# RWKV score products: each head's 64 rows alone, the two heads in turn, in place of 128 zero-padded rows

## The chip, the cores and the metric

The kernel is one program on one core of a Trainium2 chip. It has five instruction streams: PE (TensorE, matrix products; the profile shows its weight loads apart as PEld), DVE (VectorE), ACT (ScalarE), POOL (GpSimd) and SP (SyncE, which here issues nearly all DMA transfers). The metric is the device time of one execution in microseconds; less is better. The time of a kernel is the median of several runs.

## The reference

Two transformer blocks run one after the other on the same activations: 272 tokens with retention, mLSTM and 16 experts of 2816 hidden units, then 256 tokens with a gated delta net ("gdn" below), an RWKV-7 branch and 32 small experts. The second block also runs both branches over 256 context tokens, only for the state that they leave. The change is in the RWKV branch, which is this recurrence over 8 heads of 64 channels, in two directions:

```python
def rwkv7_scan(r, w, k, v, a, b, s0):
    '''S_t = S_{t-1} (diag(w_t) + a_t b_t^T) + v_t k_t^T ; y_t = S_t r_t.'''
    def step(s, inp):
        r_t, w_t, k_t, v_t, a_t, b_t = inp
        sa = jnp.einsum('...vk,...k->...v', s, a_t)
        s = s * w_t[..., None, :] + sa[..., :, None] * b_t[..., None, :] + v_t[..., :, None] * k_t[..., None, :]
        return s, jnp.einsum('...vk,...k->...v', s, r_t)
    s_fin, y = lax.scan(step, s0.astype(jnp.float32), xs)

    y, s_fin = rwkv7_scan(both_dirs(r_h), per_dir(heads(decay)), per_dir(k_dir), both_dirs(v_h),
                          both_dirs(-kk), per_dir(b_dir), s0)
```

It is run once on the context (state only, no y) and once on the 256 latent tokens, starting from the context's state.

## The kernel before

The sequence of 256 is cut in 4 chunks of 64 steps. Two heads share the 128 partitions: a pair j (0 to 3) has head h = 0 on partitions 0 to 63 and head h = 1 on 64 to 127; in the code `r` is a head's own half and `ro` the other one. For each pair and direction d:

- `rwkv_prep` and `rwkv_scale` project and scale keys, values and queries. They leave `ld` (the scaled −kk), `lw` (the scaled query, latent only), and `BK`, which holds for each chunk three blocks of 64 columns: scaled b, scaled k, scaled b again. `BK[:, c, h:h + 2, :]` is therefore (b, k) for head 0 and (k, b) for head 1.
- `rwkv_front` makes the chunk's inner products. `T[:, h, c]` is the moving operand of head h: 64 columns of `ld`, in the latent pass 64 of `lw`, and 64 of an identity that transposes. Its rows outside the head's half have to be zero, since the product contracts over all 128 partitions. Only the first 64 columns are overwritten later, so POOL sets them to zero again in each front (line 1598), DVE and ACT copy `ld` and `lw` in (lines 1599 and 1601), and PE multiplies (line 1612) into a bank `b` of PSUM that holds 4 chunks (context) or 2 (latent). Then the bank is emptied with masks: to `N` (line 1615), to the other half of `T` (line 1616), to `MR` (line 1618, latent), all on DVE, and to `BKt` on ACT (line 1619).
- `rwkv_back` inverts a unit triangular matrix made from N (`mixed_inverse`; its first products are `r0ic` and `r1ic`, line 1154, for d = 0 and 1) and walks the four chunks, each with the products of lines 1645, 1652, 1660, 1667 and 1675.

An fp32 product is two passes of the array: in the trace each matmul instruction appears as two MATMUL and two LDWEIGHTS records, in the order listings as one.

The context pass is a generator (`ctx_pre`) that runs inside the first block's experts: after a pair of expert matmuls (lines 892 and 910), `paced` advances it by as many `yield`s as are due, 470 for the first 1000 of 1050 pairs; what is left runs behind them. In the context d = 0 and d = 1 follow each other on the same tiles, with `T` in one buffer, and both use the two PSUM banks of "pb". In the latent pass d = 0 has the two banks of "pa" and d = 1 the two of "pc"; `hop(...)` (that is `fill`) issues steps of other work, projections (line 1093) and gdn products (`gic`, `gib`, `giy`), right behind the matmul that it is given, and `run` drains the generators, so that yields mean nothing there. The instructions of all this are put in their final order on each engine by a scheduler of the framework, which goes by what depends on what and by its own estimate of times. An engine then runs its list in that order. The lines of the loop in question:

```python
        for h, r, ro in self.HALF:
            for c0 in range(0, 4, cg):
                ...
                for i in range(cg):
                    ins = nc.tensor.matmul(b[:, i], BK[:, c0 + i, h:h + 2, :], T[:, h, c0 + i, :, :], start=True, stop=True)
                hop(0, HOPS[1])(ins)
```

Of the kernel before, what the change touches and what calls it, by code (L numbers as in the profile page):

```python
# [58 lines left out]
HOPS = 4, 1, (3, 1), (2, 1), (2, 1), (2, 1), (0, 4), (0, 4)  # L59
# [95 lines left out]
class Ring(list):  # L155
# [3 lines left out]
    def tile(self, *args, **kw):  # L159
        self.turn += 1  # L160
        return self[self.turn % len(self)].tile(*args, **kw)


class Net:
# [1419 lines left out]
    def rwkv_front(self, j, d, x, env):  # L1584

        nc = self.nc
        W, lat, na = env["W"], env["lat"], env["na"]
        nd = d if lat else 0
        T, N = env["T1"][nd], env["Ne"][nd]
        self.ptag = env["tags"][d]  # L1590
        ch = lambda ap: ap.rearrange("p (c t) -> p c t", c=4)
        rw = self.ct("rw").rearrange("p (d h a c) -> p d h a c", d=2, h=2, a=2)
        ld, lw, BK, wc, ic = x["scaled", d]
        tile = lambda shape, name: W.tile(shape, F32, name=f"{name}{nd}")
        hop = (lambda *steps: (lambda ins: self.fill(ins, *steps))) if lat and d == 0 else lambda *steps: (lambda ins: None)
        SU = tile([P, 2, 4, 64], "rSU")
        for h, r, ro in self.HALF:
            nc.gpsimd.memset(T[ro, h, :, 0, :], 0.0)
            nc.vector.tensor_copy(T[r, h, :, 0, :], ch(ld)[r])  # L1599
            if lat:  # L1600
                nc.scalar.copy(T[r, h, :, 1, :], ch(lw)[r])
            nc.gpsimd.tensor_scalar(SU[ro, h], x["vn"][ro], 1.0, 0.0, op0=ALU.mult, op1=ALU.add)

        BKt = tile([P, 2, 4, 64], "rKt")
        MR = tile([P, 2, 4, 64], "rMR") if lat else None
        cg = 2 if lat else 4
        for h, r, ro in self.HALF:
            for c0 in range(0, 4, cg):
                b = self.bank("rmt")[:, :cg * na * 64].rearrange("p (c a t) -> p c a t", c=cg, a=na)
                cs = slice(c0, c0 + cg)  # L1610
                for i in range(cg):
                    ins = nc.tensor.matmul(b[:, i], BK[:, c0 + i, h:h + 2, :], T[:, h, c0 + i, :, :], start=True, stop=True)  # L1612
                hop(0, HOPS[1])(ins)
                m = lambda rr, a: rw[rr, d, h, a:a + 1, :].to_broadcast([rr.stop - rr.start, cg, 64])
                nc.vector.tensor_mul(N[r, cs, r], b[r, :, 0, :], m(r, 0))
                nc.vector.tensor_mul(T[ro, h, cs, 0, :], b[ro, :, 0, :], m(ro, 0))
                if lat:
                    nc.vector.tensor_mul(MR[:, h, cs, :], b[:, :, 1, :], m(slice(0, P), 1))
                nc.scalar.copy(BKt[:, h, cs, :], b[:, :, na - 1, :])
                yield  # L1620
        return T, N, SU, BKt, MR, wc, ic

    def rwkv_back(self, j, d, x, front, env):
# [643 lines left out]
```

## Time and profile before

| | |
|---|---|
| three runs | 2544.38, 2549.94 and 2558.76 us, median 2549.94 |
| profiled execution | 2547.35 us, of which the span from first to last instruction is 2545.3 |
| TensorE clock granted, mean over the span | 0.958 of full |
| busy: PE, PEld, DVE, ACT, POOL | 2322.3, 1243.8, 1041.2, 653.8, 460.1 us |
| matmul of line 1612 | 256 records, 51.3 us busy |
| DMA | 755.05 MB, 297 GB/s over the span |

In time the program is: the first mixer (to about 300 us), the experts of the first block with the context pass inside (to 1738 us), the latent mixing stage (to about 2180 us), merging and the 32 small experts (to the end). The fronts of the change stand at 986 to 1635 us (8 of the context) and 1784 to 2096 us (8 of the latent pass). A busy share tells little by itself: matmuls are pipelined, and a record's end is modelled, so that the distance between starts is the better measure of what an instruction costs PE.

### The profile page before, as it was taken

The numbers are of one execution on the slowest core, as the hardware profiler recorded it, in microseconds if no ns is written. First come the engines' busy times: TensorE is split into PE (matmuls) and PEld (weight loads), VectorE is DVE, ScalarE is ACT, GpSimd is POOL, SyncE is SP. The second block draws the span as 40 slices with busy tenths as digits, with TensorE's granted clock in tenths as the row PEclk, the third lists the DMA queues.
The fourth block names the chain that finished last, engine by engine and source line by source line (L and its number), as shares of the span: only waits on it lengthen the run. The fifth ranks groups of instructions, "written<-read, shape, count | busy, mean of one in ns | idle before, by whom it ended". The sixth has DMA issues, their size and how long they took to land. (4 is left out here: it accounts for less than half of the span.)

```text
span 2545.3 us, 45033 instructions
## 1 busy us (share of the span) xinstructions
PE 2322.3 (91%) x18624; PEld 1243.8 (49%) x18624; DVE 1041.2 (41%) x2419; ACT 653.8 (26%) x1652; POOL 460.1 (18%) x657
## 2 busy tenths in 40 slices
PE   6879799999999999999899999997988999989997
PEld 5656533333333433333333333335766777865554
DVE  7786312232222312322322313223676464645545
ACT  4335111221121112212212112213443343522222
POOL 5672100000000101101101101103243342300000
PEclk9979899999999999999999999998888989999999
DMA  6547799999998999999999999996211112689995
GB/s 214 182 143 246 269 403 403 402 400 368 406 378 326 394 366 381 406 390 378 406 376 387 373 404 400 389 407 196 74 43 46 44 27 68 216 271 362 368 365 189
DMA packets 328176, 755.05 MB, mean 297 GB/s; under 512 B 13088, under 2 KB 167376, under 8 KB 324896
## 3 DMA queue, kind: packets, MB, share of 16 engines
q1 hardware_dynamic: 326464, 747.67, 79.5%
q0 software_dynamic: 1504, 4.46, 0.6%
q8 instruction: 149, 2.44, 0.4%
q14 instruction: 59, 0.48, 0.1%
HBM read 751.03 MB, written 1.05 MB: 295 GB/s over the span
## 5 line engine op out<-in xcount | busy, mean ns | idle before, releaser
L892 PE MATMUL gu<-w,xs 128*64 128x512 f32 (+1 forms) x3072 | 679.6, 570 | 1.6 <-DMA w<-in_w_up 1.3
L910 PE MATMUL dn<-w,hT 128*64 128x512 f32 x1408 | 336.6, 604 | 19.1 <-ACT hT L318 17.4
L892 PEld LDWEIGHTS gu<-w,xs 128*64 128x64 f32 x3072 | 195.6, 137 | 285.5 <-issue 270.6
L1093 PE MATMUL pc<-luT,w 128*128 128x256 f32 x688 | 180.7, 404 | 1.7 <-ACT r1iZ L1173 1.1
L910 PEld LDWEIGHTS dn<-w,hT 128*64 128x64 f32 x1408 | 88.8, 137 | 164.2 <-issue 131.6
L1093 PEld LDWEIGHTS pc<-luT,w 128*128 128x128 f32 x688 | 128.0, 197 | 19.7 <-ACT rSU L1664 1.2
L2123 PE MATMUL egu<-w,exs 128*64 128x256 f32 x1024 | 123.2, 383 | 0.0
L898 DVE TENSOR_TENSOR hid<-hid,gu 128x512 f32<-128x512 f32 (+1 forms) x48 | 30.7, 640 | 201.5 <-ACT hid L303 198.6
L1093 PE MATMUL pc<-cuT,w 128*128 128x256 f32 x288 | 99.2, 429 | 0.0
L1093 PEld LDWEIGHTS pc<-cuT,w 128*128 128x128 f32 x288 | 43.2, 188 | 107.8 <-issue 104.3
L2123 PEld LDWEIGHTS egu<-w,exs 128*64 128x64 f32 x1024 | 74.6, 136 | 39.4 <-issue 6.9
L1656 POOL TENSOR_SCALAR rsw<-rSU,rwc 64x64 f32<-64x64 f32 x112 | 39.8, 355 | 293.3 <-DVE rSU L1672 283.3
L301 ACT ACTIVATE hid<-gu 128x512 f32<-128x512 f32 (+1 forms) x48 | 26.9, 560 | 235.3 <-PE gu L892 235.3
L296 PE MATMUL pj<-uTh,wp 128*128 128x272 f32 x320 | 69.0, 310 | 10.7 <-DVE rtmp L469 6.4
L899 DVE TENSOR_TENSOR hid<-hid,gu 128x512 f32<-128x512 f32 (+1 forms) x48 | 30.8, 642 | 108.7 <-PE gu L892 107.1
L1612 PE MATMUL rmt<-rT,rBK 128*128 128x128 f32 (+1 forms) x256 | 51.3, 341 | 21.0 <-DVE rT L1599 13.9
L2150 PE MATMUL edn<-w,ehT 128*64 128x512 f32 x256 | 67.7, 597 | 0.7 <-ACT ehT L318 0.5
L286 ACT CAST wp<-w 128x1024 fp32r<-128x1024 f32 (+1 forms) x48 | 55.3, 1185 | 49.4 <-DMA w<-in_w_in 31.1
L287 DVE TENSOR_TENSOR wp<-w,wp 128x1024 fp32r<-128x1024 f32 (+1 forms) x44 | 62.3, 1441 | 12.2 <-ACT wp L286 12.1
L1439 POOL TENSOR_TENSOR rtm<-rpd 128x256 f32<-128x256 f32 x25 | 16.0, 640 | 273.5 <-ACT rpd L1437 264.5
L1028 POOL TENSOR_TENSOR adac<-adac,w 128x2048 f32<-128x2048 f32 x14 | 64.3, 4595 | 0.3
L1279 POOL TENSOR_TENSOR gx<-gx,gcv 128x256 f32<-128x256 f32 x20 | 14.5, 725 | 266.2 <-ACT gx L303 240.1
(680 smaller groups left out, 3678.2 us busy)
## 6 DMA issues: line engine op xcount, KB each, us to landing
w<-in_w_down SPq DMA_DIRECT2D x176, 1024.0 KB, 11.2
w<-in_w_gate SPq DMA_DIRECT2D x128, 1024.0 KB, 10.4
w<-in_w_up SPq DMA_DIRECT2D x128, 1024.0 KB, 12.1
w<-in_w_gate SPq DMA_DIRECT2D x64, 768.0 KB, 10.5
w<-in_w_up SPq DMA_DIRECT2D x64, 768.0 KB, 7.5
w<-in_w_in SPq DMA_DIRECT2D x65, 512.0 KB, 4.2
w<-in_moe_w_gate SPq DMA_DIRECT2D x32, 1024.0 KB, 13.4
w<-in_moe_w_up SPq DMA_DIRECT2D x32, 1024.0 KB, 12.0
```

What stands on the lines that cost most here:

```text
L286: self.nc.scalar.copy(hi, src)
L287: (eng or self.nc.vector).tensor_sub(lo, src, hi)
L296: self.nc.tensor.matmul(out, a[x], b[y], start=(i == 0 and x + y == 0), stop=(i == n - 1 and x == 1))
L892: ins = nc.tensor.matmul(b[h * 64:(h + 1) * 64, :w], xs[:, k, :], ws(k, slice(h * w, (h + 1) * w)), start=(k == 0), stop=(k == KD - 1))
L899: nc.vector.tensor_mul(hid, hid, gu[1][:, :w])
L910: ins = nc.tensor.matmul(dn[dc * 64:(dc + 1) * 64], hT[:, j, h * 64:(h + 1) * 64], wd(h * nf + j, slice(dc * 512, (dc + 1) * 512)), start= ...
L1028: nc.gpsimd.tensor_add(acc[c], acc[c], w)
L1093: self.nc.tensor.matmul(b, w(k), uT[:, k, :], start=(k == 0), stop=(k == KD - 1))
L1612: ins = nc.tensor.matmul(b[:, i], BK[:, c0 + i, h:h + 2, :], T[:, h, c0 + i, :, :], start=True, stop=True)
L1656: nc.gpsimd.tensor_scalar(sw[r], SU[r, h, c, :], wc[r, c:c + 1], 0.0, op0=ALU.mult, op1=ALU.add)
L2123: nc.tensor.matmul(b[64 * i:64 * i + 64, x * 256:x * 256 + 256], xs[:, k, i, :], w[i](k), start=(k == 0), stop=(k == KD - 1))
L2150: nc.tensor.matmul(b[64 * i:64 * i + 64, :], hT[:, j, 64 * i:64 * i + 64], wd[i](j, cs), start=(j == 0), stop=(j == 1))
```

## The change

The memset of line 1598 goes. The products of a head contract over its own 64 partitions only (`BK[r, ...]`, `T[r, ...]`), so that the stationary operand is 64 rows by 128 columns, in rows 0 to 63 of the array for head 0 and 64 to 127 for head 1. The loops are turned: for each group of chunks both heads' banks are taken at once, the matmuls are written chunk by chunk with the heads in turn, one `hop` of two steps stands behind all of them, then both banks are emptied, head 0 first. There is one yield for each group of chunks instead of one for each bank, that is 1 instead of 2 in a front of the context.

```diff
         for h, r, ro in self.HALF:
-            nc.gpsimd.memset(T[ro, h, :, 0, :], 0.0)
             nc.vector.tensor_copy(T[r, h, :, 0, :], ch(ld)[r])
...
-        for h, r, ro in self.HALF:
-            for c0 in range(0, 4, cg):
-                b = self.bank("rmt")[:, :cg * na * 64].rearrange("p (c a t) -> p c a t", c=cg, a=na)
-                cs = slice(c0, c0 + cg)
-                for i in range(cg):
-                    ins = nc.tensor.matmul(b[:, i], BK[:, c0 + i, h:h + 2, :], T[:, h, c0 + i, :, :], start=True, stop=True)
-                hop(0, HOPS[1])(ins)
+        for c0 in range(0, 4, cg):
+            cs = slice(c0, c0 + cg)
+
+            bs = [self.bank("rmt")[:, :cg * na * 64].rearrange("p (c a t) -> p c a t", c=cg, a=na) for _ in range(2)]
+            for i in range(cg):
+                for h, r, ro in self.HALF:
+                    ins = nc.tensor.matmul(bs[h][:, i], BK[r, c0 + i, h:h + 2, :], T[r, h, c0 + i, :, :], start=True, stop=True)
+            hop(0, 2 * HOPS[1])(ins)
+            for h, r, ro in self.HALF:
+                b = bs[h]
                 m = lambda rr, a: rw[rr, d, h, a:a + 1, :].to_broadcast([rr.stop - rr.start, cg, 64])
                 nc.vector.tensor_mul(N[r, cs, r], b[r, :, 0, :], m(r, 0))
                 nc.vector.tensor_mul(T[ro, h, cs, 0, :], b[ro, :, 0, :], m(ro, 0))
                 if lat:
                     nc.vector.tensor_mul(MR[:, h, cs, :], b[:, :, 1, :], m(slice(0, P), 1))
                 nc.scalar.copy(BKt[:, h, cs, :], b[:, :, na - 1, :])
-                yield
+            yield
```

PE's order in the fourth front of the context, before. `rmt` with its number is a bank of the product (of the two here the smaller number is head 0), `gu` and `dn` are the experts' banks, `r0ic` the first product of the inverse.

```order
L910 MATMUL dn_8090<-w_8202,hT_8194 64x512 x4
L1612 MATMUL rmt_8265<-rT0_6140,rBK0_8246 128x128 x4
L892 MATMUL gu_8273<-w_8274,xs_7851 64x512 x4
L1612 MATMUL rmt_8286<-rT0_6140,rBK0_8246 128x128 x4
L892 MATMUL gu_8273<-w_8276,xs_7851 64x512 x4
L1154 MATMUL r0ic_8309<-r0iB_8299 32x32 x16
```

The same place now:

```order
L903 MATMUL hb_8220<-ctab_64,hid_8214 128x128 x4
L910 MATMUL dn_8101<-w_8227,hT_8225 64x512 x4
L1612 MATMUL rmt_8243<-rT0_6140,rBK0_8205 128x128 x4
L1612 MATMUL rmt_8244<-rT0_6140,rBK0_8205 128x128 x4
L910 MATMUL dn_8101<-w_8229,hT_8225 64x512 x4
L910 MATMUL dn_8101<-w_8231,hT_8225 64x512 x4
L1154 MATMUL r0ic_8274<-r0iB_8264 32x32 x16
```

The eight products stand together, the four of head 0 ahead of the four of head 1; the heads are not in turn. Seven of the eight fronts of the context read so.

PE's order in the last front of the context, now:

```order
L892 MATMUL gu_10750<-w_10753,xs_10345 64x512 x2
L1612 MATMUL rmt_10791<-rT0_6140,rBK0_10774 128x128
L1612 MATMUL rmt_10792<-rT0_6140,rBK0_10774 128x128
L1612 MATMUL rmt_10791<-rT0_6140,rBK0_10774 128x128
L1612 MATMUL rmt_10792<-rT0_6140,rBK0_10774 128x128
L1612 MATMUL rmt_10791<-rT0_6140,rBK0_10774 128x128
L1612 MATMUL rmt_10792<-rT0_6140,rBK0_10774 128x128
```

Here alone the heads are in turn, as the loop writes them (the two rows that follow go on in the same way).

PE's order in the latent front of pair 1, d = 0, before. `rp13` and `rp24` are banks of the walk over the chunks, `pc` a projection, `gic` a product of the gdn inverse. The four banks of a front are, by rising number, head 0 with chunks 0 and 1, head 0 with 2 and 3, then head 1 in the same way; of them two are shown.

```order
L1675 MATMUL rp13_12651<-rSU0_12086,rMR0_12096 64x64
L1612 MATMUL rmt_12984<-rT0_11707,rBK0_12522 128x192 x2
L1093 MATMUL pc_12675<-luT_11601,w_11646 128x256
L1154 MATMUL gic_15474<-giB_15427 32x32 x2
L1645 MATMUL rp13_12883<-rSU1_12132,rT1_11708 64x64 x2
L1612 MATMUL rmt_12992<-rT0_11707,rBK0_12522 128x192 x2
L1093 MATMUL pc_12675<-luT_11601,w_11646 128x256
L1154 MATMUL gic_15474<-giZ_15428,giB_15427 32x32 x13
```

The same place now; by rising number the banks are head 0 and head 1 with chunks 0 and 1, then head 0 and head 1 with 2 and 3:

```order
L1677 MATMUL rp13_12631<-rSU0_12070,rMR0_12078 64x64
L1612 MATMUL rmt_12962<-rT0_11691,rBK0_12502 128x192 x2
L1647 MATMUL rp13_12863<-rSU1_12114,rT1_11692 64x64
L1154 MATMUL gic_15442<-giB_15395 32x32 x13
L1612 MATMUL rmt_12963<-rT0_11691,rBK0_12502 128x192 x2
L1093 MATMUL pc_12655<-luT_11585,w_11630 128x256 x2
...
L1612 MATMUL rmt_12978<-rT0_11691,rBK0_12502 128x192 x2
L1612 MATMUL rmt_12979<-rT0_11691,rBK0_12502 128x192 x2
L1093 MATMUL pc_12655<-luT_11585,w_11630 128x256 x2
```

A bank's two products still stand together, and other products mostly stand between the two heads' banks; in this front the second group has them next to each other.

## Rows read from the trace of the kernel before

**Rows 1.** Busy time by stretch: length, five engines (instructions), clock, DMA share, GB/s.
```profile
core 0: us, PE busy (x) PEld busy (x) DVE busy (x) ACT busy (x) POOL busy (x), PEclk, DMA share, GB/s
1440.00:1460.00 20.00, 18.38 (x204) 6.97 (x202) 6.01 (x16) 2.55 (x8) 2.63 (x4) 0.93 0.85 318
...
1500.00:1520.00 20.00, 19.15 (x84) 6.30 (x82) 1.25 (x3) 0.60 (x1) 0.48 (x2) 1.00 1.03 409
...
1720.00:1740.00 20.00, 14.96 (x77) 4.70 (x73) 3.19 (x6) 2.91 (x6) 0.97 (x1) 0.99 1.07 363
```

**Rows 2.** PE's waits, 330 to 1740 us: for whom, us in all, times, longest.
```profile
PE rmt L1612 <- DVE rT L1599: 13.9, 6, 3.1
...
PE r0ic L1154 <- POOL r0iB L1169: 3.0, 3, 1.7
...
PE gu L892 <- DMA w<-in_w_up: 1.3, 3, 0.5
```

**Rows 3.** Timeline of PE, two fronts of the context: start, length, what, records.
```profile
1252.17 1.16 PE L1612 MATMUL rmt<-rT,rBK 128*128 128x128 f32 x8
...
1253.26 1.94 PE L892 MATMUL gu<-w,xs 128*64 128x512 f32 x8
...
1375.12 2.05 PE L1612 MATMUL rmt<-rT,rBK 128*128 128x128 f32 x16
1377.10 4.09 PE L892 MATMUL gu<-w,xs 128*64 128x384 f32 x24
```

**Rows 4.** Timeline of PE: 64-row products in turn, and a stream of 128-row ones.
```profile
1666.54 0.73 PE L924 MATMUL sc<-yhi,ohT 64*128 64x512 f32 x4 [0.69 <-ACT yhi L918]
1667.20 1.08 PE L892 MATMUL gu<-w,xs 128*64 128x512 f32 x4
...
2294.70 4.10 PE L2084 MATMUL exg<-eohq,exp 128*128 128x256 f32 x32
2298.64 0.38 PE L2114 MATMUL ecb<-ctab,eohp 128*128 128x128 f32 x2
```

**Rows 5.** Groups of PE, 1745 to 2180 us: records, busy us, mean ns, idle before.
```profile
L1093 PE MATMUL pc<-luT,w 128*128 128x256 f32 x622 | 165.5, 406 | 1.1 <-ACT r1iZ L1173 1.1
L1612 PE MATMUL rmt<-rT,rBK 128*128 128x192 f32 x128 | 32.7, 391 | 7.2 <-ACT rT L1601 4.4 <-ACT rKt L1619 2.8
```

**Rows 6.** PE's waits, 1740 to 2180 us.
```profile
PE rp L1645 <- DVE rSU L1672: 8.0, 5, 4.3
PE rp L1675 <- DVE rSU L1664: 6.8, 4, 5.0
```

**Rows 7.** Timeline of all engines in the latent front of pair 1.
```profile
1882.96 0.92 PE L1612 MATMUL rmt<-rT,rBK 128*128 128x192 f32 x4
...
1883.72 0.59 PE L1093 MATMUL pc<-luT,w 128*128 128x256 f32 x2
...
1884.37 0.28 DVE L1615 TENSOR_TENSOR rN<-rmt,stab 64x128 f32<-64x128 f32 x1
...
1884.67 0.29 DVE L1616 TENSOR_TENSOR rT<-rmt,stab 64x128 f32<-64x128 f32 x1
...
1884.97 0.29 DVE L1618 TENSOR_TENSOR rMR<-rmt,stab 128x128 f32<-128x128 f32 x1
```

**Rows 8.** Busy time by stretch, latent stage, columns as in rows 1.
```profile
1797.80:1865.80 68.00, 65.10 (x820) 50.79 (x818) 37.34 (x95) 34.52 (x96) 17.74 (x32) 1.00 0.33 88
...
1893.30:1906.80 13.50, 13.50 (x214) 10.22 (x215) 7.53 (x28) 4.57 (x15) 5.29 (x12) 0.50 0.15 40
1958.20:1975.00 16.80, 11.72 (x80) 8.74 (x80) 12.80 (x29) 4.73 (x14) 6.45 (x8) 0.50 0.11 31
2006.00:2012.60 6.60, 5.39 (x53) 4.03 (x54) 3.40 (x10) 0.46 (x2) 0.45 (x1) 0.50 0.01 2
```

**Rows 9.** The memset of line 1598: ns min/median/max; what POOL waited for before it.
```profile
L1598 POOL MEMSET rT<- x32: 304/306/450, 887.0 to 2083.8; 64x256 f32 x32
...
  PE rp L1645: 13.2, 10
```

## The prediction, on record before the changed kernel ran

> **What bounds the kernel now.** I read the busy time by stretch first, for which engine or queue is full where, then PE's waits in the two stages that the change touches, then the timeline around single fronts, and last the granted clock of the latent stage.
>
> The experts of the first block, with the context pass among them, run between two full resources. Where nothing disturbs, PE is busy 19.15 of 20 us and DMA moves 409 GB/s at a share of 1.03; where a context front and the inverse behind it stand, DMA falls to 318 GB/s and 0.85, since PE frees weight buffers late; in the last 20 us of the stage, with the context done, PE is busy only 14.96 and DMA is full [rows 1]. Over the whole stage PE waits 1.3 us for weights, but 13.9 us, six times, for the copy into T ahead of the product, and 3.0 us for the first product of the inverse [rows 2]. So a microsecond that PE saves in a context front is part of a stage whose end waits for weights: some of it comes through, not all.
>
> In the latent stage little is loaded (88 GB/s in one stretch) and PE is busy 65.10 of 68 us [rows 8]; what it waits for are single late steps of the chunk walk, 8.0 and 6.8 us in all [rows 6]. There PE's time counts nearly in full. What matters as much is its clock: three stretches of 6.6 to 16.8 us were granted 0.50, the lower of its two levels (1.2 GHz), beside 68 us at 1.00 (2.4 GHz) [rows 8].
>
> **The change, part by part.** The first question is what a product costs. A front's 16 records of 128 columns take from 1375.12 to 1377.10 us, 1.98 us, and 8 of them from 1252.17 to 1253.26, 1.09 us [rows 3]. Two equations: 0.111 us a record and 0.20 us for entering and leaving. In the latent pass 4 records of 192 columns take 0.76 us until the next product starts [rows 7], 0.19 each; by columns from the context's it would be 0.167 (an estimate, 192/128 of 0.111). All 128 latent records are 32.7 us busy [rows 5], some of them at the lower clock.
>
> Contracting over 64 rows in place of 128 removes no record and no column. Time is gained only if the two halves of the array work at once. That this can be so is in the trace [rows 4]: four passes of 64 rows, halves in turn, 512 columns each, take from 1666.54 to 1667.20, 0.66 us. The passes over 128 rows with operands of the same type take 3.94 us for 32 of 256 columns, 0.123 each, so four of 512 would take 0.98 one after the other.
>
> But the order that PE gets decides whether neighbours lie in different halves, and it is not the loop's. The scheduler puts a bank's products together: in seven of the eight context fronts four of head 0, then four of head 1; in every latent front two of one head, then, mostly behind other work, two of the other. Products of one head use the same rows and follow each other. Only at a seam, where the last of head 0 stands next to the first of head 1, can two overlap.
>
> - Seams. Context: 7 fronts, one product (two records) hidden in each, 7 x 2 x 0.111 = 1.6 us; the last front alternates, 8 x 0.111 = 0.9. Sum -2.5 us. Latent: PE's list has three places where the heads' banks touch, 3 x 2 x 0.167 = -1.0 us.
> - Visits. A context front was two visits to PE between expert products, now it is one; one of the eight was one before. 7 x 0.20 = -1.4 us. In the latent fronts I count neighbours with another tile shape in PE's list: 31 at either end of the product's rows before, 56 now, since a projection, 128 by 128, was of the same shape and no longer is. Over the whole stretch from the first front to the last the list changes shape 357 times before and 356 now. So the price lies between 0 and 25 x 0.10 = 2.5 us (half a visit each); I take +1.0.
> - The drain. The Trainium skill, TensorEngine Tiling (Array Packing), section Tiling Modes, says that changing the tiling mode, unlike changing the tile, drains TensorE; the 0.20 us from [rows 3], between products of 64-column tiles, agree. By the rule as it stands the 25 added edges all pay; by the count over the whole list none is added.
> - Waits in the context. Between the products of `rbw` and a front's first product the list now has up to 12 expert products where it had 8 or 10, in three of the fronts, and a pair of them is worth about 0.9 us (half of the 1.94 us in [rows 3]). 13.9 us [rows 2] could shrink by 3; against that one front has only four expert products ahead of its inverse in place of ten. Bounds -3 and +3, taken -1.0.
> - Emptying. The same six DVE operations for a pair of banks, 0.28 to 0.29 us each [rows 7], and the ACT copies. Head 0's half of N is complete after the third bank and no longer after the second; the inverse needs both heads, and head 1 was last before too. Taken 0. If the last two banks come together, three operations of head 0 stand ahead of head 1's N: 0.9 us a front, +7 us over the eight latent fronts if nothing else were late; PE has other products to run meanwhile, which is what hides it.
> - The memset. 32 x 0.306 = 9.8 us of POOL go, and 13.2 us in which POOL stood before it, waiting for a product [rows 9]. What stood behind it on POOL, copies into SU and the scaling `rsw`, waits for the same walk over the chunks. Bounds 0 and -5, taken -0.3.
> - The generator. Eight fewer yields of the context end it some 17 expert pairs earlier (8 of 470 steps of 1000 pairs). That lengthens the stretch in which PE waits for weights anyway [rows 1]: 0.
>
> Sum. Context on PE: -2.5 - 1.4 - 1.0 = -4.9 us, of which I pass on a quarter, since the stage ends on full DMA [rows 1]: -1.2. Latent: -1.0 + 1.0 - 0.3 = -0.3. Together -1.5 on the profiled execution's 2547.35 us: 2545.9, said as 2546. That execution is 2.6 us below the median of the three runs, 2549.94, whose spread is 14 us. I call 0.5%, 12.7 us, what a measurement of this kernel can tell from no change, so faster means below 2537.2 and slower above 2562.7.
>
> **The rivals.**
>
> The halves overlap after all. If the array ran both heads side by side as the loop writes it, a context front would lose 8 x 0.111 = 0.9 us and the latent fronts 64 x 0.167 = 10.7 us, more at the lower clock. For it: the four passes of [rows 4], and the latent stage pays PE's time in full. Against it: the order. With a quarter of the context's 8 x 0.9 + 1.4 = 8.6 us, and the latent sum, it gives 2547.35 - 10.7 - 2.2 = 2534.
>
> The clock, which is the rival on the slower side. A latent stretch of 13.5 us at 0.50 in which PE has work, such as 1893.30 to 1906.80 with PE busy throughout [rows 8], costs half its length, 6.75 us. It begins just behind a latent front. Products on half the rows, and a list in which 25 more edges break the stream, could make PE look less active there. One stretch more gives 2553, two 2559, three 2566; it decides from the third on. Against it: as many columns pass as before, and the stretches at 0.50 may as well become fewer, by which the same step gives 2539.
>
> The drains and the late N. All 25 edges at 0.20 us, 5 us, and a part of the 7 us of emptying: 2552. For it: the 0.20 us of [rows 3]. Against it: the unchanged count over the list.
>
> **How the numbers follow.** No overlap but at seams, 2546: 0.58 (of it 0.05 faster, 0.02 slower, by a shuffled latent order). Overlap, 2534: 0.14 (0.10 faster, the rest within). Clock, 2553 to 2566: 0.13 (0.10 slower). Drains, 2552: 0.15 (0.01 slower). Faster 0.15, same 0.72, slower 0.13. The range takes in the overlap's 2534 and the clock's second step: 2534 to 2560. The likeliest case's own range is 2539 to 2553, one stretch of the clock either way.
>
> **What would show it.** The records of line 1612: still 256, now of shape 64 by 128. In a context front the start of the next product stands about 1.75 us behind the first (16 records less two, and one visit); 1.1 us would show the overlap, as it should in the last front. In the latent pass two products of one head should still take 0.6 us or more. Wrong would be the forecast if the product's busy time fell by a third or more in the latent stage, if the stretches at 0.50 there grew by more than two, or if PE's waits for DMA at the end of the experts moved that stage's end by over 5 us.

## The result, and the profile after

The changed kernel takes 2568.29 us (median of 5 runs, 2566.36 to 2573.14) against 2553.13 for the kernel before (5 runs, 2544.38 to 2558.76). The ratio on record is 1.0077, 95% interval 1.0057 to 1.0096 (the quotient of the two medians is 1.0059): slower, beyond the 0.5% that was called what a measurement can tell. The forecast was 2546 with a range from 2534 to 2560; the measured time lies above it.

The profiled execution took 2571.5 us, 24.2 us more than the profiled one before. Three marks that both traces have cut it in parts: the first expert product (`gu`), the last product `sc` of the first block's experts, and the last `afT` product of the second block. Up to the first mark the changed kernel is 4.2 us later, in code that the change doesn't touch; over all the profiles of this study that mark lies anywhere from 311.8 to 319.2 us. From the first mark to the second, the stage with the context pass, 1424.6 us stand against 1424.4. From the second to the third, the latent stage, 537.4 against 517.3: here are the 20.1 us. Behind it the two agree within 0.1 us.

Busy time of the latent stage as one stretch (columns: stretch, length, busy us of PE, PE's weight loads, DVE, ACT and POOL with their instructions, mean granted clock of TensorE, DMA share, GB/s), first of the kernel before, then of the changed one:

```profile
1738.50:2255.80 517.30, 471.81 (x5727) 381.99 (x5724) 307.41 (x812) 218.82 (x637) 171.68 (x286) 0.91 0.30 88
```

```profile
1742.90:2280.30 537.40, 496.37 (x5728) 395.96 (x5724) 304.30 (x812) 220.21 (x637) 164.48 (x270) 0.87 0.28 85
```

PE has the same instructions (5727 and 5728 records) and is busy 24.6 us longer; its idle time (length less busy) fell from 45.5 to 41.0 us. So it is not waiting that grew: PE does the same work more slowly, and the mean clock says why, 0.87 in place of 0.91. Added up from the trace's stretches, the time granted 0.50 went from 92.2 to 143.4 us. Half of the 51.2 us between them, 25.6, is what PE loses if it has work all the while; 24.6 is what its busy time shows. Counted at full clock, as the busy time at 1.00 (399.2 us before, 367.5 after) and half of that at 0.50 (72.6 and 128.9), PE's work in the stage is 435.5 us before and 431.9 after: it did not grow. It is not more stretches, eight in either kernel, but longer ones: the longest was 17.1 us, now there are one of 37.5 and one of 44.4. Stretches of the changed kernel, to be read beside [rows 8]:

```profile
1899.90:1937.40 37.50, 37.07 (x486) 25.80 (x487) 18.77 (x63) 10.39 (x35) 10.12 (x20) 0.50 0.06 17
1937.40:1985.30 47.90, 45.62 (x560) 35.85 (x559) 29.83 (x79) 22.97 (x67) 15.42 (x29) 1.00 0.22 59
1985.30:2029.70 44.40, 43.92 (x549) 34.29 (x550) 23.46 (x82) 11.15 (x41) 16.17 (x31) 0.50 0.06 15
```

The reader is to see PE busy 37.07 of 37.50 us and the lower of the two levels, 1.2 GHz, all the same. The Trainium skill, TensorE: Matmul & The Clock Gate, Part 1, says that activity releases a throttle that is on by default, and describes the activity as how busy the PE has been. This trace agrees with the first half, as both long stretches end inside full-array products (below). If busy is read as having an instruction, the trace differs from the second: PE had one for 0.99 of a stretch that stayed at 0.50.

The same place in both kernels, the second front of pair 1, on PE's timeline (start, length, what, shape of the stationary operand, of the moving one, records). Before:

```profile
1902.55 1.65 PE L1612 MATMUL rmt<-rT,rBK 128*128 128x192 f32 x4
1903.99 1.92 PE L1182 MATMUL gib<-giZ,giN 128*128 128x128 f32 x8
1905.84 0.42 PE L1154 MATMUL r0ic<-r0iZ,r0iB 32*32 32x32 f32 x10
1906.19 1.24 PE L1612 MATMUL rmt<-rT,rBK 128*128 128x192 f32 x4
```

After:

```profile
1914.40 1.65 PE L1612 MATMUL rmt<-rT,rBK 64*128 64x192 f32 x4
1915.97 0.36 PE L1154 MATMUL gic<-giB 32*32 32x32 f32 x9
...
1933.46 1.65 PE L1182 MATMUL gib<-giZ,giN 128*128 128x128 f32 x6
1934.90 4.90 PE L1093 MATMUL pc<-luT,w 128*128 128x256 f32 x16
```

Before, the clock rose at 1906.9, within this front, behind its first four records and the full-array products `gib`. After, the whole front (1914.3 to 1924.4) passed at 0.50, and the clock rose only at 1937.4, inside a run of full-array products, `gib` and the projections of line 1093. The long stretch that ended at 2029.7 ended the same way, inside 16 such records. And the lines price a product: at 0.50 four front records take 1.44 us until the next product starts before, 1.57 after.

The rest of the profile went much as it was read. Groups of PE, 1745 to 2180 us, answering [rows 5] (records, busy us, mean ns, idle before); fewer projections fall into this window, as the stage starts later and lasts longer:

```profile
L1093 PE MATMUL pc<-luT,w 128*128 128x256 f32 x560 | 153.8, 417 | 0.0
L1612 PE MATMUL rmt<-rT,rBK 64*128 64x192 f32 x128 | 37.9, 462 | 7.2 <-ACT rT L1600 4.4 <-ACT rKt L1621 2.8
```

PE's waits in the latent stage, answering [rows 6] (lines have moved by two): the 8.0 us for `rSU` became 4.7, the 6.8 us 1.4, and a wait for `rys` came in their place.

```profile
PE ryt L1713 <- DVE rys L1708: 6.4, 1, 6.4
PE rp L1647 <- DVE rSU L1674: 4.7, 2, 4.3
...
PE rp L1677 <- DVE rSU L1666: 1.4, 1, 1.4
```

And the experts' stage with the context, PE's waits from 330 to 1740 us, answering [rows 2], then one context front, answering [rows 3]:

```profile
PE rmt L1612 <- DVE rT L1598: 11.1, 6, 2.2
...
PE gu L892 <- DMA w<-in_w_up: 3.2, 7, 0.6
```

```profile
992.81 1.68 PE L1612 MATMUL rmt<-rT,rBK 64*128 64x128 f32 x16 [2.20 <-DVE rT L1598]
994.42 0.65 PE L892 MATMUL gu<-w,xs 128*64 128x512 f32 x2
```

A context front takes 1.61 us in place of 1.98, and PE waits 2.8 us less for T. The stage is not shorter for it: PE's busy time in it is 1333.2 us before and 1333.5 after, its idle time 91.2 and 91.1. The wait for weights grew from 1.3 to 3.2 us, and 27.3 us of the stage were granted 0.50 in place of 20.4. Over all the profiles of this study the stage takes 1422.6 to 1429.1 us, so that a gain of a microsecond or two could not be seen in one of them.

### The profile page after: what moved, and what is told of

Read it like the earlier page. It is cut to its first block, busy times and chain, and to the rows that moved or that the text cites. A ratio compares the mean times of both kernels' runs of the same rounds, so it can differ in the third digit from the quotient of the medians.

```text
span 2569.7 us, 44986 instructions
## 1 busy us (share of the span) xinstructions
PE 2347.6 (91%) x18624; PEld 1256.0 (49%) x18624; DVE 1046.9 (41%) x2419; ACT 652.5 (25%) x1652; POOL 447.9 (17%) x625
## 5 line engine op out<-in xcount | busy, mean ns | idle before, releaser
L898 DVE TENSOR_TENSOR hid<-hid,gu 128x512 f32<-128x512 f32 (+1 forms) x48 | 30.8, 642 | 233.4 <-ACT hid L303 230.6
L1093 PEld LDWEIGHTS pc<-cuT,w 128*128 128x128 f32 x288 | 43.2, 188 | 107.4 <-issue 104.7
L899 DVE TENSOR_TENSOR hid<-hid,gu 128x512 f32<-128x512 f32 (+1 forms) x48 | 30.8, 641 | 114.1 <-PE gu L892 113.9
L1612 PE MATMUL rmt<-rT,rBK 64*128 64x128 f32 (+1 forms) x256 | 51.6, 375 | 18.3 <-DVE rT L1598 11.1
```

What stands on the lines that cost most here:

```text
L898: nc.vector.tensor_mul(hid, hid, gu[0][:, :w])
L1093: self.nc.tensor.matmul(b, w(k), uT[:, k, :], start=(k == 0), stop=(k == KD - 1))
L1612: ins = nc.tensor.matmul(bs[h][:, i], BK[r, c0 + i, h:h + 2, :], T[r, h, c0 + i, :, :], start=True, stop=True)
```

## The experiments

Ten kernels ran, in three groups; each group had its own runs of the kernel before beside it (medians 2547.15, 2548.32 and 2548.13 us). The latent stage is measured between the same two marks throughout. "At 0.50" is the sum of the stretches granted that level in it; it and the three columns before it are read from one profile of each kernel.

| kernel | rows in context / latent | median us | ratio, interval | latent us | PE busy | PE idle | at 0.50 |
|---|---|---|---|---|---|---|---|
| before | 128 / 128 | – | 1 | 517.3 | 471.8 | 45.5 | 92.2 |
| after | 64 / 64 | 2568.29 | 1.0077 (1.0057–1.0096) | 537.4 | 496.4 | 41.0 | 143.4 |
| old_half | 64 / 64 | 2573.32 | 1.0115 (1.0098–1.0132) | 541.3 | 496.4 | 44.9 | 133.1 |
| old_half_nomemset | 64 / 64 | 2568.55 | 1.0086 (1.0070–1.0103) | 541.8 | 499.9 | 41.9 | 139.9 |
| new_full_memset | 128 / 128 | 2548.62 | 1.0009 (0.9995–1.0024) | 519.3 | 473.5 | 45.8 | 92.2 |
| half_lat | 128 / 64 | 2567.38 | 1.0076 (1.0054–1.0098) | 537.4 | 496.3 | 41.1 | 143.4 |
| half_ctx | 64 / 128 | 2546.94 | 0.9992 (0.9981–1.0004) | 516.4 | 465.0 | 51.4 | 64.9 |
| alt_ctx | 64 in forced turns / 128 | 2548.39 | 1.0013 (0.9994–1.0033) | 515.3 | 465.4 | 49.9 | 64.9 |
| alt_both | 64 in forced turns / same | 2559.65 | 1.0053 (1.0035–1.0071) | 527.7 | 480.7 | 47.0 | 119.5 |
| after_extra | 64 / 64, and 32 full products | 2576.95 | 1.0127 (1.0110–1.0144) | 545.7 | 502.5 | 43.2 | 112.6 |
| after_twice | 64 / 64 issued twice | 2576.90 | 1.0107 (1.0069–1.0146) | 546.3 | 503.4 | 42.9 | 116.1 |
| warm_idle | 128 / 128, and 28 full products | 2556.07 | 1.0037 (1.0021–1.0054) | 522.9 | 479.9 | 43.0 | 85.3 |

One profile's time at 0.50 is not exact. new_full_memset and half_ctx give PE the same list of latent instructions (5721 of 5724 in the same order) and show 92.2 and 64.9 us. So the clock of every run belongs beside the column. Its mean over the whole program is 0.954 to 0.964 in 51 runs of the kernel before. It is 0.946 to 0.951 in all 17 runs of the four kernels with half rows in the latent pass and nothing forced or added there (after, old_half, old_half_nomemset, half_lat), 0.952 to 0.954 in after_extra, 0.947 to 0.957 in after_twice and 0.949 to 0.955 in alt_both. PE's work counted at full clock, as above, is 430.1 to 439.0 us in the nine kernels that add no products, whatever their clock.

**Rows or loops.** The change has two parts that can stand alone: the rows that a product works on, and the loops that turn from head to head. Three kernels fill the square.

old_half and old_half_nomemset, from the kernel before (the second without the memset of line 1598 too):

```
-  ins = nc.tensor.matmul(b[:, i], BK[:, c0 + i, h:h + 2, :], T[:, h, c0 + i, :, :], start=True, stop=True)
+  ins = nc.tensor.matmul(b[:, i], BK[r, c0 + i, h:h + 2, :], T[r, h, c0 + i, :, :], start=True, stop=True)
```

> The loops of before with 64 rows in each product in place of 128 (memset kept). Theory A (clock by rows: a product on half the rows works half the array, so that the clock in the latent stage rises later): 2560 to 2570 us, more than 110 us of the latent stage at 0.50. Rival B (order: the turned loop and the head-wise groups cost the time, rows do not matter): 2550 to 2556 us and 70 to 90 us at 0.50, as before.

> The loops of before with 64 rows and without the memset. Theory A: 2558 to 2570 us, more than 110 us of the latent stage at 0.50. Rival B: 2548 to 2556 us. If only this one of the two is slow, it is the memset's going that reorders the latent stage.

new_full_memset, from the changed kernel:

```
+  nc.gpsimd.memset(T[ro, h, :, 0, :], 0.0)
...
-  ins = nc.tensor.matmul(bs[h][:, i], BK[r, c0 + i, h:h + 2, :], T[r, h, c0 + i, :, :], start=True, stop=True)
+  ins = nc.tensor.matmul(bs[h][:, i], BK[:, c0 + i, h:h + 2, :], T[:, h, c0 + i, :, :], start=True, stop=True)
```

> The turned loops of the change with all 128 rows and the memset kept. Theory A: 2546 to 2557 us, at most 95 us of the latent stage at 0.50. Rival B: 2562 to 2572 us, as the change.

The rows decide. With the old loops and half rows, 2573.32 (3 us more than the theory had named) and 2568.55; with the new loops and full rows, 2548.62, an interval that holds 1. The latent stage of old_half, of old_half_nomemset, then of new_full_memset:

```profile
1737.20:2278.50 541.30, 496.40 (x5728) 393.88 (x5724) 306.94 (x812) 219.98 (x637) 172.70 (x286) 0.88 0.28 84
```

```profile
1739.40:2281.20 541.80, 499.87 (x5727) 396.15 (x5724) 305.11 (x812) 220.03 (x637) 166.78 (x270) 0.87 0.28 84
```

```profile
1737.20:2256.50 519.30, 473.54 (x5728) 382.87 (x5724) 306.53 (x812) 219.44 (x637) 173.80 (x286) 0.91 0.29 87
```

One thing these kernels do not hold fixed is PE's order in the latent stage, since the scheduler makes it anew for each. Of the 5723 records that start in it in the kernel before, 4344 stand in the same order in old_half, though one line was edited, and 4887 in new_full_memset; old_half and the changed kernel have 4605 in common. Full rows keep the time in two orders and half rows lose it in two, which speaks for the rows. No run has half rows in the very order of the kernel before.

Whether the memset itself is worth anything is not told apart: the intervals of the two kernels with the old loops overlap, and their latent stages differ by 0.5 us.

**Context or latent.** From the changed kernel, `lat` being true in the latent pass; half_lat has `lat` where half_ctx has `not lat`, and the zeroing stays where rows are full:

```
+  q = r if not lat else slice(0, P)
-  ins = nc.tensor.matmul(bs[h][:, i], BK[r, c0 + i, h:h + 2, :], T[r, h, c0 + i, :, :], start=True, stop=True)
+  ins = nc.tensor.matmul(bs[h][:, i], BK[q, c0 + i, h:h + 2, :], T[q, h, c0 + i, :, :], start=True, stop=True)
```

> The changed loops; context products on half the rows, latent products over all 128 rows with the zeroing kept there. Theory A (the latent stage loses its clock when its front products work on half the rows): the latent stage stands as before, at most 100 us of it at 0.50, and the total is 2543 to 2553 us. Rival C (half-row products cost time wherever they stand, by their edges with other tile shapes): 2552 to 2560.

> The changed loops; latent products on half the rows, context products over all 128 with the zeroing kept there. Theory A: 2562 to 2575 us, over 120 us of the latent stage at 0.50, which is all that the change lost. Rival C: about half to three quarters of the loss, 2555 to 2563.

The whole loss is the latent pass's: half_lat has the latent stage of the changed kernel to 0.1 us and its total; half_ctx has the time of before. The rival that edges between tile shapes cost wherever they stand, which had half_ctx at 2552 or more, falls.

```profile
1739.10:2276.50 537.40, 496.32 (x5728) 396.05 (x5724) 304.25 (x812) 220.24 (x637) 164.41 (x270) 0.87 0.28 85
```

```profile
1743.70:2260.10 516.40, 465.04 (x5728) 376.90 (x5724) 307.66 (x812) 219.06 (x637) 172.83 (x286) 0.94 0.29 88
```

The second row, of half_ctx, sets a bound on the theory. It has 27.3 us less at 0.50 than the kernel before, 13.7 us' worth, and the stage is 0.9 us shorter: PE is busy 6.8 us less and idle 5.9 more. So time at 0.50 is not always time lost: here most of what PE gained it spent waiting. What held the stage then, perhaps the walk over the chunks on DVE and ACT, was not tested.

**Is it the clock, or narrow products as such?** Two kernels give work in the array back without taking the half rows away. after_extra, from the changed kernel, one full-array product into each latent front bank, overwritten by the real ones:

```
+  if lat:
+      for b in bs:
+          nc.tensor.matmul(b.rearrange("p c a t -> p (c a t)")[:, :256], self.ident, self.ct("rw")[:, :256], start=True, stop=True)
```

> The changed kernel with one product of 128 rows, 128 columns of weights and 256 columns more into each bank of a latent front, written over by the real ones: 32 products, 0.21 us each at the full clock, 7 us of work added. Theory A: the clock stays up or rises earlier, 2545 to 2560 us, faster than the change in spite of the work. Rival B: 2568 plus 3 to 9, 2571 to 2577 us.

after_twice, from the changed kernel:

```
+  if lat:
+      for i in range(cg):
+          for h, r, ro in self.HALF:
+              ins = nc.tensor.matmul(bs[h][:, i], BK[r, c0 + i, h:h + 2, :], T[r, h, c0 + i, :, :], start=True, stop=True)
   hop(0, 2 * HOPS[1])(ins)
```

> The changed kernel with every latent front product issued a second time into the same place, with the same values, so that as many rows times columns pass as with 128 rows. By the front's 36.0 us for 128 records in the changed kernel the repeat costs 25 to 36 us. Theory A: the clock comes back for part of it, at most 120 us of the latent stage at 0.50 (143 now), and the total is 2570 to 2592. Rival C (narrow tiles and their edges are slow, the clock only follows): 140 us or more at 0.50 and 2593 to 2606.

after_extra's total is the figure that the rival had named, 2577, and 17 us above the theory's range; read by the total alone it would have felled the theory. The trace says otherwise: the time at 0.50 fell from 143.4 to 112.6 us. What the expectation had wrong was the price of the addition, 7 us. The 32 products are 64 records that hold PE for 24.2 us (from the start of one to the start of the next, or to its own end where PE then waits), 12.2 at full clock and 12.0 at 0.50, which is 18.2 us at full clock. At that price the rival would have had to name some 2586; this was worked out afterwards. Less half of the 30.8 us, 15.4, the addition should lengthen the stage by 2.8 us; it is 8.3 longer, and the 5.5 between were not followed up. Against the kernel before, 18.2 us and half of 20.4 us more at 0.50 make 28.4, and the stage is 28.4 us longer. after_twice adds 128 records that hold PE for 25.3 us, 19.8 at full clock, and has 27.3 us less at 0.50: 19.8 - 13.7 = 6.1 by the same sum, 8.9 measured. Its total and its 116.1 us lie within what the theory had named and outside what the rival had.

```profile
1738.50:2284.20 545.70, 502.52 (x5792) 395.46 (x5788) 302.30 (x812) 219.47 (x637) 165.39 (x270) 0.90 0.28 83
```

```profile
1742.90:2289.20 546.30, 503.42 (x5856) 407.34 (x5852) 304.77 (x812) 219.45 (x637) 165.88 (x270) 0.89 0.28 83
```

With the added work taken off at full clock, the stages come to 527.5 and 526.5 us, 9 to 10 us above before, where half of their 20 to 24 us more at 0.50 is 10 to 12. That leaves the narrow product next to no price of its own. The 128 records of the latent fronts, measured in the same way, show it directly: at full clock 0.193 us each before (99 records, 19.1 us) and 0.202 after (61, 12.3); at 0.50 0.346 before (29, 10.0) and 0.353 after (67, 23.7). With full rows in the new loops they are 0.199 and 0.357 (new_full_memset), so that not even this small rise is the rows' for certain. The fronts hold PE for 36.0 us in place of 29.1 nearly all because more of them runs at 0.50.

**The order that the loop writes.** The list that PE gets had four products of one head together. alt_both forces the turns; alt_ctx does so in the context alone, with full rows in the latent pass.

```
+  ins = None
   for i in range(cg):
       for h, r, ro in self.HALF:
+          with self.tc.issue_after(ins.ins) if ins else ExitStack():
               ins = nc.tensor.matmul(bs[h][:, i], BK[r, c0 + i, h:h + 2, :], T[r, h, c0 + i, :, :], start=True, stop=True)
```

> The changed kernel, with the products of the two heads forced to be issued in turn (head 0, head 1, head 0, ...) instead of four of one head and then four of the other. Theory A: the products lie over each other, a context front takes 0.8 to 1.1 us from first to last start instead of 1.41 to 1.44, which the experts' stage hides, and in the latent stage even less of the array is at work in a stretch: 140 us or more at 0.50, total 2556 to 2572. Rival D (the change lost only because the order was not the one meant): 2535 to 2550, latent time at 0.50 under 120 us. If the products don't lie over each other, fronts stay at 1.4 us and the total at 2565 to 2575.

> Half rows in the context only, where the products of the two heads are forced to be issued in turn; latent products over all 128 rows in the changed loops, the zeroing kept there. The forced turns shorten context fronts by 0.2 to 0.5 us each, which the experts' stage, full on DMA, hides for the most part. Theory A: the latent stage is left as before, total 2542 to 2549 us against before's 2548. Rival C (each edge of a half-row front costs): 2550 to 2557.

The products do lie over each other. A context front of alt_both:

```profile
1239.10 1.16 PE L1614 MATMUL rmt<-rT,rBK 64*128 64x128 f32 x16
1240.19 0.65 PE L910 MATMUL dn<-w,hT 128*64 128x512 f32 x2
```

It takes 1.09 us to the next product's start, and so does one other front; the other six take 1.43 to 1.82. From first to last start the eight take 0.89 to 1.48 us (the expectation had 0.8 to 1.1 for all). In the latent stage the turns take back half of the loss, with the fronts at 28.0 us of PE and 119.5 us at 0.50; 140 or more was expected, so that number was wrong, and the rival's, under 120, was met. The total of 2559.65 lies in the theory's range and not in the rival's, and still above before: half rows, even side by side, leave the clock lower than full rows do.

```profile
1740.70:2268.40 527.70, 480.67 (x5727) 382.09 (x5724) 304.77 (x812) 219.46 (x637) 166.26 (x270) 0.89 0.29 86
```

alt_ctx joins what was best of each, and is not told apart from the kernel before: the stage with the context takes 1428.0 us, no less than before, and the latent stage 515.3, about what half_ctx has. No version here beats the kernel before.

**Raising the clock from idle time.** warm_idle, from the kernel before: full-array products that nobody reads, put ahead of three of PE's waits.

```
+  for _ in range(n):
+      with self.tc.issue_after(ins.ins) if ins else ExitStack():
+          ins = self.nc.tensor.matmul(bk[:, 256:512], self.ident, self.ct("rw")[:, :256], start=True, stop=True)
```

> The kernel before with 28 products of 256 columns over 128 rows, whose results nobody reads, put where its latent stage waits anyway: 9 ahead of the first front (PE idle for 4.4 us there), 9 ahead of the third chunk step of pair 0 (4.3 us), 10 behind the third step's second product of pair 1 (5.0 us). At about 0.43 us each they are 12 us at full clock. Theory A: full-array work raises the clock behind it, at most 85 us of the latent stage at 0.50 (92 before), and since most of the work lies in waits the total is 2538 to 2550. Rival E (what is at work in the array does not set the clock): 92 us or more at 0.50, total 2548 to 2560 by what isn't hidden.

Inconclusive as a whole: 85.3 us at 0.50 is the theory's number nearly, but within what one list of instructions showed by itself (64.9 and 92.2), and 2556.07 is the rival's. Of the three groups, the one ahead of the third chunk step waited for `rSU` itself, 4.3 us, so that its work came behind the wait and not in it; and the order of much that follows changed. Where the first group lay as meant, the clock followed: the stretch that began at 1784.0 in the kernel before and lasted 13.7 us lasts 3.4. That may be in part chance, since half_ctx, without the added products, has 3.4 and 6.8 us there.

```profile
1787.00:1798.50 11.50, 8.10 (x46) 6.97 (x45) 11.33 (x32) 3.23 (x9) 7.71 (x11) 1.00 0.17 46
1798.50:1801.90 3.40, 3.40 (x12) 3.14 (x11) 3.29 (x15) 2.71 (x10) 0.73 (x1) 0.50 0.02 5
```

## Why the prediction was wrong

**The step that failed** is that the sum has no term for the clock. The likeliest case, 2546 with 0.58, leaves the granted clock of the latent stage as it was, but for one stretch either way; the clock stood among the rivals with 0.13, and the reason given against it was "as many columns pass as before". As many columns do pass, but each through half the rows, and the runs show that this counts: one line that halves the rows adds 40.9 us at 0.50 (old_half), passing the half rows twice takes 27.3 of the 51.2 away, full-array products 30.8. The term put at nothing measured 51.2 us more at 0.50, and the latent stage, forecast at -0.3, lost 20.1. That PE was busy in almost all of a stretch at 0.50 stood in [rows 8] already, PE busy 13.50 of 13.50 us; it should have told that being busy does not by itself keep the clock up, and that the width of what PE does had to be asked about.

The rival's mechanism, its place and its price were right: half rows make PE look less active in the latent stage, and a stretch at 0.50 costs about half its length. Its form was not: it counted further stretches of 13.5 us, and the trace has eight as before, two of them much longer. Its last step named 2566, and 2568.29 was measured; as nothing in it said how many steps there would be, coming so close is luck.

**The sum's terms**, one after the other. Seams and visits in the context: a front was forecast at about 1.75 us to the next start and took 1.61 to 1.64 in six of the seven, since three records, not two, start beside others; the last, alternating front, forecast at 1.1, took 1.52. Of the quarter of the context's gain that was passed on, 1.2 us, nothing is to be seen (1424.6 us against 1424.4, in a stage that varies by 6.5 from profile to profile), nor in the totals of half_ctx and alt_ctx. Waits in the context: the copy into T, 13.9 to 11.1 us, as forecast in sign, and made up at other places. Seams and visits in the latent stage, -1.0 and +1.0: the records' own price at either clock rose by 0.007 to 0.009 us, 128 of them about 1 us; the two terms were not told apart. The Trainium skill, TensorEngine Tiling (Array Packing), section Key Properties, has two statements here: a change of tiling mode drains TensorE, and different tiles run in parallel. The second is what the forced turns show (16 records in 1.09 us in place of 1.98 in the best fronts). For the first, 25 more edges and about 1 us leave little room. The rival of the drains, which had 5 us for the edges, is not what happened. Emptying and the late N: no such wait among the first of the latent stage. The memset: POOL's busy time fell from 460.1 to 447.9 us, and no time with it that the runs can tell.

**The other rival**, overlap by itself, was rightly rejected by the order, and alt_both shows what it would have met: even with the turns forced the kernel is 0.5% slower than before.

**The sign.** Faster had 0.15, same 0.72 and slower 0.13. The forecast priced PE's time, found it unchanged, and treated the clock as something that happens beside it, while the clock depended on just what the change altered.

**What stays open.** The sum by the clock is not exact from kernel to kernel: the loss of the latent stage is 0.8 of half the time added at 0.50 in the changed kernel, 1.0 in old_half_nomemset, 1.2 in old_half, and in half_ctx a gain of 13.7 us arrived as 0.9. Waits of PE that open or close take up part of the difference (its idle time lies between 41.0 and 51.4 us); which of them does in each kernel was not followed up. Nor was the share of the scheduler's new order held apart from that of the rows.

## What to carry to other kernels

When an edit leaves PE's instructions and columns as they are but makes them narrower, look at the granted clock of that stage before calling it free: here the stage was near full on PE and already fell to 0.50 now and then, and with narrower products two of those stretches became two to three times as long. Read an added or removed piece of work by two sums, what it holds PE for at full clock and half of the change in time at 0.50, since the total alone can point the wrong way. A gain on PE is worth something only where PE is late: the context's fronts became about a fifth shorter, and in forced turns up to 45%, for nothing that the runs can tell.

## What the runs showed of the hardware

- Rows of the array that multiply zeros kept the clock up. In the kernel before, half of the moving operand's rows in a front product are zeros; leaving these rows out by one edited line, with the order that the scheduler then made, took the latent stage from 92.2 to 133.1 us at 0.50 (old_half).
- At 0.50 PE worked at about half the pace: a front record held it for 0.193 us at 1.00 and 0.346 at 0.50 in the kernel before, and its busy time in the latent stage, counted in full at 1.00 and half at 0.50, is 430.1 to 439.0 us in nine kernels with 64.9 to 143.4 us at 0.50.
- Products on the two halves of the rows overlap without being issued strictly in turn: of eight records of one head followed by eight of the other, the front took 1.61 us, 0.37 less than over full rows; in strict turns 1.09 us in two of eight fronts and 1.43 to 1.82 in the others.
- The same latent list of PE instructions ran with 92.2 us at 0.50 in one kernel (new_full_memset) and 64.9 in another (half_ctx), and the stage differed by less than the clock would make it: 519.3 and 516.4 us.
